# Stick-breaking attention with pooling: the closing's stores and the weight sums on GpSimd's queue, loads spread out

## The chip, the cores and the metric

One core of a Trainium2 chip. The metric is device time in microseconds; the profile beside it is one execution, recorded by the hardware profiler.

## The reference

One layer with two token mixers runs over 2048 prompt rows and 64 decode rows (each 1024 wide), everything in fp32:

```python
def merge_out(x, att, ga, pb, gb, mg, w_br_a, w_br_b, w_out):
    y_a = (att * jax.nn.silu(ga)) @ w_br_a
    y_b = (pb * jax.nn.silu(gb)) @ w_br_b
    gate = jax.nn.sigmoid(mg)
    m = gate[..., :D_MODEL] * y_a + gate[..., D_MODEL:] * y_b
    return x + m @ w_out
...
        h = rmsnorm(xp, norm_g[l])
        q, k, v, ga, u, gb, mg = split_proj(h, w_in[l])
        att = stick_breaking(...)      # 8 heads x 128, strictly causal
        pb = multi_scale_pool(...)     # trailing means of 2/4/8/16 rows minus self, a map per group
        xp = merge_out(xp, att, ga, pb, gb, mg, w_br_a[l], w_br_b[l], w_out[l])
...
    y_prompt = rmsnorm(xp, final_g)
```

`split_proj` is one projection to 8192 columns; `att` is written out as keys and values too. The change is about `merge_out`: the three products with `w_br_a`, `w_br_b` and `w_out`, and the gates.

## The kernel before

Every fp32 product is made of three products of rounded halves: `split` casts a tile to `hi` on ScalarE (L81) and takes `lo = src - hi` on VectorE (L82); TensorE then sums hi·hi, hi·lo and lo·hi (`product`, L964, L966, L968).

The program has three parts. First, projections and attention (to about 2267 us in the profile) leave three arrays in DRAM: `aT_d` and `bT_d`, the two branches' rows after their own gates, transposed, and `sm_d`, the merge gates after the sigmoid. Second, the closing (2267 to 2648): for branch i = 0 (`w_br_a`) and i = 1 (`w_br_b`), three row tiles t of 2 x 352 rows. Third, the back: `w_out` over eight pairs of 128-row blocks, residual and final norm, then the decode rows.

The three large products are done with seven block products in place of eight (Winograd's form of Strassen's scheme), p = 0 to 6, with weights `b11, b21, t2, t1, t3, b22, t4`. The `t` are sums of weight blocks: `weight_sums` loads four 128x512 pieces (`ws`, L899), subtracts four times (L902) and stores four times to `tw_d` (L903), twelve rounds in all (three weights by four k). They run beside the last projection slabs; there a planner spaces the steps of `before_closing` between slabs, and instructions of engines other than TensorE are put in an order by a scheduler. A slab is 128 columns of `w_in`: two loads `raw` (L272) of 256 KB, `whi` and `wlo` from them, 48 matmuls of 128x512 and a few narrower, and the sigmoid's stores `sm_d` (L306).

In the closing, every engine's order is written out by hand, and is the order of the code. A row tile needs `r11, r12, r21, r22` (128x4x352 each, L1044) and four sums of them. A product p is two half steps cc of 24 matmuls of 128x352 into an accumulator; a tile is 14 half steps, the closing 84 (h = 2s + cc, with s counting products). `make(s + 2)` splits the rows of the product after the next into `rhi` and `rlo`. Some results are kept by ScalarE (L979: `x1`, `x2`, `x5`); the other eight of a tile go through `emit`: add a kept result (L1103), multiply with the gate `sg` (L1105), in branch 1 add branch 0's result `mp` (L1107). The tile `sg` is then stored to `mp_d` (branch 0) or `m_d` (branch 1) by `store`, half a step later on SP (L1091), and behind it SP issues the load of `mp` for the result after the next (L1085) and of the gate four results ahead (L1078), whose tile is the one just stored. `forms` loads a weight in two pieces of 512 KB (`wraw`, two buffers, L914) and splits them; each `next(wnext)` does one piece and starts the load of the piece after the next.

In the back, a product is 12 matmuls of 128x512 and a pair has seven. `out_a` to `out_d` make the forms of a pair's rows, `join` adds results to the residual `xo` (L1204, L1205), `finish` norms and stores. `mt` and `mb` hold a pair's rows from `m_d`.

Of the kernel before, what the change touches and what calls it, by code (L numbers as in the profile page):

```python
# [15 lines left out]
P = 128  # L16
D = 1024
# [27 lines left out]
def kernel(  # L45
# [99 lines left out]
    with ExitStack() as front:  # L145
# [747 lines left out]
        def weight_sums(i):  # L893

            for k in range(4):
                t = {}
                for nm, r, c in (("b11", 0, 0), ("b12", 0, 1), ("b22", 1, 1), ("b21", 1, 0)):
                    t[nm] = kept_tile("ws").rearrange("p a b -> p (a b)")[:, 0:512]
                    nc.sync.dma_start(t[nm], weights[i][r * 512 + k * P:r * 512 + (k + 1) * P, c * 512:(c + 1) * 512])  # L899
                for j, out, x, y in ((0, "b11", "b12", "b11"), (2, "b12", "b22", "b12"),  # L900
                                     (1, "b22", "b22", "b11"), (3, "b21", "b21", "b22")):
                    nc.vector.tensor_tensor(t[out], t[x], t[y], op=ALU.subtract)  # L902
                    nc.sync.dma_start(tw_d[i, j, k * P:(k + 1) * P, :], t[out])  # L903
                yield 1.0
# [81 lines left out]
    def load_merged(n):  # L986

        r0 = pairs[n][0]
        for h in range(2):
            nc.sync.dma_start(merged[n][h], m_d[h * 512:(h + 1) * 512, r0:r0 + 256].rearrange("(k p) r -> p k r", p=P))  # L990

# [15 lines left out]
    def out_b(n, s1, s2):  # L1007
        r11, r12, r21, r22 = blocks(n)
        s1, s2 = s1[:, :, 0:P], s2[:, :, 0:P]
# [16 lines left out]
    with ExitStack() as rowx, tc.manual_schedule(engines={E.PE, E.DVE, E.Activation, E.SP}):  # L1026
# [7 lines left out]
        stores = []  # L1034

        def load_rows(s, nm):
            if s >= len(order):
                return
# [6 lines left out]

        def sum12():

            raws["s1"] = rowp.tile([P, 4, NR], F32, name="s1")
            raws["s2"] = rowp.tile([P, 4, NR], F32, name="s2")
            nc.vector.tensor_tensor(raws["s1"], raws["r21"], raws["r22"], op=ALU.add)  # L1050
            nc.vector.tensor_tensor(raws["s2"], raws["s1"], raws["r11"], op=ALU.subtract)

        def sum34():

            nc.vector.tensor_tensor(raws["r21"], raws["r11"], raws["r21"], op=ALU.subtract)
            nc.vector.tensor_tensor(raws["r12"], raws["r12"], raws["s2"], op=ALU.subtract)

        def make(s):

            if s < len(order):  # L1060
                rf[s] = row_form()
                split(rf[s][0], rf[s][1], raws[("r11", "r12", "s2", "s1", "r21", "r12", "r22")[order[s][2]]])

            elif s == len(order):
                out_a(0)
            else:
                out_b(0, rowp.tile([P, 4, NR], F32, name="s1"), rowp.tile([P, 4, NR], F32, name="s2"))
# [5 lines left out]
        def load_gate(n):  # L1073
            if n < len(leave):
                i, c, rs = where(n)
                sgs_[n] = rowp.tile([P, 2, NR], F32, name="sg", bufs=4)
# [3 lines left out]
        def load_other(n):  # L1080

            if n < len(leave) and leave[n][0]:
                i, c, rs = where(n)
                mps[n] = rowp.tile([P, 2, NR], F32, name="mp", bufs=2)
                nc.sync.dma_start(mps[n], mp_d[c * P:(c + 2) * P, rs].rearrange("(j p) r -> p j r", p=P))  # L1085

        def store():
            while stores:
                n = stores.pop(0)
                i, c, rs = where(n)  # L1090
                nc.sync.dma_start((mp_d, m_d)[i][c * P:(c + 2) * P, rs].rearrange("(j p) r -> p j r", p=P), sgs_.pop(n))  # L1091
                load_other(n + 2)
                load_gate(n + 4)
# [3 lines left out]
        def emit(src, other):  # L1097
# [3 lines left out]
            sg = sgs_[n]  # L1101
# [4 lines left out]
            if leave[n][0]:  # L1106
                nc.vector.tensor_tensor(sg, sg, mps.pop(n), op=ALU.add)  # L1107
            return n

        for nm in ("r21", "r22", "r11", "r12"):  # L1110
            load_rows(0, nm)
        for n in range(4):
            load_gate(n)
        wnext = forms(0, WFORMS[4:])
        next(wnext)
        sum12()
        for s, (i, t, p) in enumerate(order):
            r = rf.pop(s)
            if t == 2 and p == 0:
                wnext = forms(i + 1, WFORMS)  # L1120
            for cc in range(2):
# [9 lines left out]
                if cc == 1:  # L1131
                    make(s + 2)
                out = acc[:, :, 0:NR]
                n = None
                if p == 0:
                    x1[cc] = kept(out, "x1")
                elif p == 1:
                    n = emit(out, x1[cc])
# [4 lines left out]
                elif p == 4:  # L1143
                    n = emit(out, x5[cc])
                elif p == 5:
                    n = emit(out, x2[cc])
                else:
                    n = emit(out, None)
                if p == 0 and cc == 1:
                    sum34()  # L1150
                if p == 6 and cc == 1 and s + 1 < len(order):
                    sum12()
                store()
                if n is not None:
                    stores.append(n)
                if p == 4 and cc == 1:
                    for nm in ("r11", "r21", "r12") if s + 3 < len(order) else ():
                        load_rows(s + 3, nm)
                    if s + 3 == len(order):
                        merged[0] = [rowp.tile([P, 4, NR], F32, name=nm)[:, :, 0:256] for nm in ("r11", "r21")]  # L1160
                        load_merged(0)
                if p == 5 and cc == 0:
                    load_rows(s + 2, "r22")
                next(wnext, None)
        store()
        for _ in wnext:
            pass
# [3 lines left out]
    with ExitStack() as back:  # L1171
        pool = back.enter_context(tc.tile_pool(name="back", bufs=1, side="left"))
        wo = {nm: wf[2, nm] for nm in WFORMS}
        left, right, whole, cols = slice(0, 512), slice(512, 1024), slice(0, 512), slice(0, P)

        def fetch(n):
            if n < len(pairs):
                merged[n] = [pool.tile([P, 4, 256], F32, name=nm, bufs=2) for nm in ("mt", "mb")]
                load_merged(n)

        def residual(src, m):
            xt = pool.tile([P, D], F32, name="xo", bufs=4)
            nc.sync.dma_start(xt[0:m], src)
            return xt

        def finish(xt, m, dst):

            acc = [pool.tile([P, 1], F32, name=f"acc{i}", bufs=2) for i in range(4)]
            for b in range(2):
                jk = pool.tile([P, 512], F32, name="bjk", bufs=2)  # L1190
                nc.scalar.activation(jk[0:m], xt[0:m, b * 512:(b + 1) * 512], AF.Square, accum_out=acc[b][0:m])
            nc.vector.tensor_tensor(acc[0][0:m], acc[0][0:m], acc[1][0:m], op=ALU.add)
            rs = pool.tile([P, 1], F32, name="rs", bufs=2)
            rsqrt_of_mean(rs[0:m], acc[0][0:m], [acc[2][0:m], acc[3][0:m]])
            for b in range(2):
                bs = slice(b * 512, (b + 1) * 512)
                nc.vector.scalar_tensor_tensor(xt[0:m, bs], xt[0:m, bs], rs[0:m], g_bc[0:m, bs],
                                               op0=ALU.mult, op1=ALU.mult)
                nc.sync.dma_start(dst[:, bs], xt[0:m, bs])

        def join(xt, bs, ps, other):

            if other is not None:
                nc.vector.tensor_tensor(xt[:, bs], xt[:, bs], other, op=ALU.add)  # L1204
            nc.vector.tensor_tensor(xt[:, bs], ps, xt[:, bs], op=ALU.add)  # L1205

        fetch(1)
        xts = [residual(xp[pairs[0][1] + i * P:pairs[0][1] + (i + 1) * P], P) for i in range(2)]
        g_bc = pool.tile([P, D], F32, name="fg_bc")
        nc.sync.dma_start(g_bc, final_g.rearrange("(a d) -> a d", a=1).broadcast_to([P, D]))  # L1210
        for n, (_, r) in enumerate(pairs):
            f = {nm: of.pop((n, nm)) for nm in ("a11", "a12", "s2", "s1", "a22")}
            last = n + 1 == len(pairs)
            xs2 = bpsum.tile([P, 2, 512], F32, name="x")
            ys2 = bpsum.tile([P, 2, 512], F32, name="y")
            x, z, y = xs2[:, 0], ys2[:, 0], ys2[:, 1]
            product(x, f["a11"], wo["b11"], True, cols, whole)
# [87 lines left out]
```

## Time and profile before

| what | us |
|---|---|
| three runs, median (range) | 2851.36 (2848.66 to 2851.92) |
| the profiled execution | 2851.63 |
| its span | 2849.9 |
| TensorE busy in the span | 2728.8 |
| closing, first to last matmul | 2267.1 to 2648.5 |
| end of the span | 2849.9 |

The span runs from the first to the last recorded instruction. A row of a timeline gives start, length, engine, line, operation, `out<-in`, and in brackets the idle time before it with the instruction or transfer that ended it. SPq is SyncE's queue, which issues DMAs. PEclk is the clock that TensorE was granted, 1.00 being full.

### The profile page before, as it was taken

What the parts mean: (1) busy time and instruction counts of PE and PEld (TensorE: products, weight loads), DVE (VectorE), ACT (ScalarE), POOL (GpSimd) and SP (SyncE); (2) the same over time, 40 slices, a digit from 0 to 9 for tenths busy, and PEclk for the clock granted to TensorE, in tenths of its full rate; (3) what the DMA queues carried; (4) which work ended last, traced back from release to release, by engine and by line L of the source; (5) the groups of instructions that cost most, each with busy time, mean ns of one, the idle gap of its engine ahead of it and who ended that gap; (6) DMA issues with size and microseconds to landing.
All of it is one profiled execution on the core that took longest, in us unless ns stands there. A gap on an engine that the chain in (4) does not pass through costs nothing.

```text
span 2849.9 us, 41818 instructions
## 1 busy us (share of the span) xinstructions
PE 2728.8 (96%) x15052; PEld 2380.2 (84%) x15052; DVE 1848.5 (65%) x2931; ACT 1270.9 (45%) x2528; POOL 444.0 (16%) x1091
## 2 busy tenths in 40 slices
PE   6999999999999999999999999999999999798798
PEld 6989888889998988788888888887778889798686
DVE  6555555677768773678788878874444265656686
ACT  4446444455555543455555555552223132323343
POOL 2112222220000002132333333420000000000000
PEclk9999999999999999999999999999999999999899
DMA  5224222234544453211111111123369555657652
GB/s 149 70 86 123 70 73 75 82 113 149 161 154 149 148 161 119 60 53 42 54 58 52 46 56 57 35 72 101 105 225 300 196 185 168 210 171 225 209 171 92
DMA packets 360315, 343.85 MB, mean 121 GB/s; under 512 B 30174, under 2 KB 298190, under 8 KB 360108
## 3 DMA queue, kind: packets, MB, share of 16 engines
q1 hardware_dynamic: 360108, 341.19, 38.4%
q8 instruction: 118, 1.93, 0.3%
q14 instruction: 89, 0.73, 0.1%
HBM read 232.46 MB, written 108.65 MB: 120 GB/s over the span
## 4 chain that ended last, share of the span: by engine, by line
PE 81%; DMA 8%; DVE 6%; issue 2%; ACT 2%; SPq 1%; POOL 0%; DVEq 0%; ACTq 0%; POOLq 0%
PE pj L284 16%; PE pj L286 16%; PE pj L285 16%; PE tr L638 4%; PE att L655 2%; PE att L654 2%; PE z L627 2%; PE att L653 2%; PE z L626 2%; PE z L625 2%; PE x L964 2%; PE x L966 2%; PE x L968 2%; PE y L964 1%; PE y L968 1%
## 5 line engine op out<-in xcount | busy, mean ns | idle before, releaser
L284 PE MATMUL pj<-hhi,whi 128*128 128x512 f32 (+2 forms) x2608 | 946.7, 363 | 5.0 <-ACT whi L81 5.0
L286 PE MATMUL pj<-hhi,wlo 128*128 128x512 f32 (+2 forms) x2608 | 919.5, 353 | 0.5 <-DVE wlo L82 0.5
L285 PE MATMUL pj<-hlo,whi 128*128 128x512 f32 (+2 forms) x2608 | 918.0, 352 | 0.1
L284 PEld LDWEIGHTS pj<-hhi,whi 128*128 128x128 f32 x2608 | 495.3, 190 | 64.8 <-ACT whi L81 5.9
L286 PEld LDWEIGHTS pj<-hhi,wlo 128*128 128x128 f32 x2608 | 493.0, 189 | 66.8 <-DVE wlo L82 1.8
L285 PEld LDWEIGHTS pj<-hlo,whi 128*128 128x128 f32 x2608 | 494.5, 190 | 59.0 <-DVE hlo L82 0.4
L579 DVE TENSOR_TENSOR_SCAN om<-om 128x513 f32<-128x513 f32 (+3 forms) x356 | 387.5, 1088 | 213.4 <-POOL om L561 108.5
L569 ACT ACTIVATE om<-z 128x512 f32<-128x512 f32 (+2 forms) x320 | 171.6, 536 | 323.2 <-PE z L627 274.4
L82 DVE TENSOR_TENSOR wlo<-raw,whi 128x512 fp32r<-128x512 f32 x248 | 170.6, 694 | 135.5 <-ACT whi L81 134.6
L582 DVE TENSOR_TENSOR be<-be,om 128x512 f32<-128x512 f32 (+3 forms) x356 | 230.2, 647 | 31.5
L81 ACT CAST whi<-raw 128x512 fp32r<-128x512 f32 x256 | 158.1, 623 | 173.9 <-PE pj L285 135.5
L81 ACT CAST a<-tr 128x512 fp32r<-128x512 f32 (+2 forms) x356 | 188.0, 528 | 100.3 <-PE tr L638 89.6
L82 DVE TENSOR_TENSOR a<-tr,a 128x512 fp32r<-128x512 f32 (+2 forms) x356 | 215.2, 605 | 23.8 <-ACT a L81 21.6
L581 POOL COPY carry<-om 128x1 f32<-128x1 f32 x356 | 78.6, 221 | 920.7 <-DVE om L579 880.3
L638 PE MATMUL tr<-ident,be 128*128 128x128 f32 x1088 | 176.0, 274 | 6.1 <-DVE be L582 3.7
L638 PEld LDWEIGHTS tr<-ident,be 128*128 128x128 f32 x1088 | 136.5, 140 | 44.9 <-DVE be L582 8.3
L570 ACT ACTIVATE be<-z 128x512 f32<-128x512 f32 (+2 forms) x320 | 170.0, 531 | 0.0
L653 PE MATMUL att<-a,v 128*128 128x512 f32 (+1 forms) x320 | 133.4, 417 | 0.0
L574 POOL COPY om<-carry 128x1 f32<-128x1 f32 x224 | 124.0, 554 | 2.7 <-DVE be L582 0.7
L655 PE MATMUL att<-a,v 128*128 128x512 f32 (+1 forms) x320 | 118.4, 370 | 3.6 <-DVE a L82 3.3
L654 PE MATMUL att<-a,v 128*128 128x512 f32 (+1 forms) x320 | 117.3, 367 | 0.0
L627 PE MATMUL z<-khi,qlo 128*128 128x512 f32 (+2 forms) x320 | 117.1, 366 | 0.0
(313 smaller groups left out, 4544.4 us busy)
## 6 DMA issues: line engine op xcount, KB each, us to landing
raw<-in_w_in_dram SPq DMA_DIRECT2D x256, 256.0 KB, 3.2
sg<-sm_d SPq DMA_DIRECT2D x48, 352.0 KB, 3.3
kraw<-in_cache_k_dram SPq DMA_DIRECT2D x64, 256.0 KB, 3.5
vraw<-in_cache_v_dram SPq DMA_DIRECT2D x64, 256.0 KB, 2.9
sm_d<-sgm SPq DMA_DIRECT2D x48, 256.0 KB, 2.7
tw_d<-ws SPq DMA_DIRECT2D x48, 256.0 KB, 3.0
wraw<-tw_d SPq DMA_DIRECT2D x24, 512.0 KB, 4.7
out_dram<-nat SPq DMA_DIRECT2D x42, 256.0 KB, 2.3
```

The source lines that it names most:

```text
L81: nc.scalar.copy(hi, src)
L82: (nc.gpsimd if eng == "g" else nc.vector).tensor_tensor(lo, src, hi.bitcast(F32), op=ALU.subtract)
L284: nc.tensor.matmul(ps[:, 0:n], whi[:, k], hhi[:, k, c0:c0 + n], start=k == 0, stop=False)
L285: nc.tensor.matmul(ps[:, 0:n], whi[:, k], hlo[:, k, c0:c0 + n], start=False, stop=False)
L286: nc.tensor.matmul(ps[:, 0:n], wlo[:, k], hhi[:, k, c0:c0 + n], start=False, stop=k == KT - 1)
L579: nc.vector.tensor_tensor_scan(rev, rev, rev, 1.0, op0=ALU.mult, op1=ALU.bypass)
L582: nc.vector.tensor_tensor(be[:, off:512], be[:, off:512], om[:, off + 1:513], op=ALU.mult)
L627: nc.tensor.matmul(z[:, off:512], qlo[:, qs], khi[:, 0:m], start=False, stop=True)
L638: nc.tensor.transpose(tr[:, i * P:(i + 1) * P], be[:, off + j * P:off + (j + 1) * P], ident)
L653: nc.tensor.matmul(self.acc[:, s], vhi[:, js], ahi[:, s], start=first, stop=False)
L654: nc.tensor.matmul(self.acc[:, s], vlo[:, js], ahi[:, s], start=False, stop=False)
L655: nc.tensor.matmul(self.acc[:, s], vhi[:, js], alo[:, s], start=False, stop=last)
```

## The change

- `weight_sums` issues its loads and stores on GpSimd's queue instead of SP's.
- `emit` issues its own store, on GpSimd's queue, and behind it the load of `mp` two results ahead and of the gate three ahead (before: four ahead, half a step later, behind the store). There are five `sg` and three `mp` buffers (before four and two), in a pool of their own that outlives the row tiles.
- In a half step, results are kept or emitted first; `make` and the sums follow. The sums are done in place, except `s3`.
- The next tile's rows are loaded at four places of the tile: `r11` at p = 2, `r21` at p = 3, `r12` and `r22` in the two halves of p = 5 (before: three at the end of p = 4, the fourth in p = 5). At the start: three row loads, three gates, the fourth row load; the weights `t3, b22, t4` follow from half step 2.
- Weight forms are placed by half step: branch 0's last six at 5 to 10 (before from 0), branch 1's fourteen at 30 to 50 (before 28 to 41), `w_out`'s at 71 to 84.
- The row tiles are given up at half step 79; the back's first rows (`mt`, `mb`) and residuals are loaded there. `mt`, `mb` and `bjk` have one buffer, and pair n + 1's rows are fetched within pair n after `out_c` (before: two pairs ahead). The back's accumulators, and the two of the decode rows, are separate tiles. The final gains lie in two of the `sg` tiles, `s1` and `s2` in `mp` tiles.

```diff
-                    nc.sync.dma_start(t[nm], weights[i][...])
+                    nc.gpsimd.dma_start(t[nm], weights[i][...])
...
-                    nc.sync.dma_start(tw_d[i, j, k * P:(k + 1) * P, :], t[out])
+                    nc.gpsimd.dma_start(tw_d[i, j, k * P:(k + 1) * P, :], t[out])
...
+        def sum3():
+            raws["s3"] = rowp.tile([P, 4, NR], F32, name="s3")
+            nc.vector.tensor_tensor(raws["s3"], raws["r11"], raws["r21"], op=ALU.subtract)
         def sum12():
-            raws["s1"] = rowp.tile([P, 4, NR], F32, name="s1")
-            raws["s2"] = rowp.tile([P, 4, NR], F32, name="s2")
-            nc.vector.tensor_tensor(raws["s1"], raws["r21"], raws["r22"], op=ALU.add)
-            nc.vector.tensor_tensor(raws["s2"], raws["s1"], raws["r11"], op=ALU.subtract)
-        def sum34():
-            nc.vector.tensor_tensor(raws["r21"], raws["r11"], raws["r21"], op=ALU.subtract)
-            nc.vector.tensor_tensor(raws["r12"], raws["r12"], raws["s2"], op=ALU.subtract)
+            nc.vector.tensor_tensor(raws["r21"], raws["r21"], raws["r22"], op=ALU.add)
+            nc.vector.tensor_tensor(raws["r11"], raws["r21"], raws["r11"], op=ALU.subtract)
+        def sum4():
+            nc.vector.tensor_tensor(raws["r12"], raws["r12"], raws["r11"], op=ALU.subtract)
...
-        def store():
-            while stores:
-                n = stores.pop(0)
-                i, c, rs = where(n)
-                nc.sync.dma_start((mp_d, m_d)[i][...], sgs_.pop(n))
-                load_other(n + 2)
-                load_gate(n + 4)
...
             nc.vector.tensor_tensor(sg, src, sg, op=ALU.mult)
-            if leave[n][0]:
+            if i:
                 nc.vector.tensor_tensor(sg, sg, mps.pop(n), op=ALU.add)
-            return n
+            nc.gpsimd.dma_start((mp_d, m_d)[i][...], sg)
+            load_other(n + 2)
+            load_gate(n + 3)
...
+        for base, nms, at in ((2, WFORMS[4:], [5, 6, 7, 8, 9, 10]),
+                              (28, WFORMS, [30 + (8 * h) // 5 for h in range(14)]),
+                              (70, WFORMS, list(range(71, 85)))):
...
-                if cc == 1:
-                    make(s + 2)
                 out = acc[:, :, 0:NR]
...
-                if p == 4 and cc == 1:
-                    for nm in ("r11", "r21", "r12") if s + 3 < len(order) else ():
-                        load_rows(s + 3, nm)
...
+                if cc == 1:
+                    make(s + 2)
+                    if p == 0:
+                        sum4()
+                    if more and p == 5:
+                        sum3()
+                    if more and p == 6:
+                        sum12()
+                weights_at(2 * s + cc)
+                if more and (p, cc) in ((2, 0), (3, 0), (5, 0), (5, 1)):
+                    load_rows(s + 7 - p, {2: "r11", 3: "r21", 5: ("r12", "r22")[cc]}[p])
+                if not more and (p, cc) == (4, 1):
+                    rowx.close()
+                    pool = ctx.enter_context(tc.tile_pool(name="back", bufs=1, side="left"))
+                    fetch(0)
+                    xts = residuals(0)
...
+        g_bc.append(gates.tile([P, 2, NR], F32, name="fg_bc", tag="sg", bufs=5)...)
...
+    def accumulator(nm):
+        return bpsum.tile([P, 2, 512], F32, name=nm)[:, 0]
...
             join(xts[0], left, z, x1)
+            if not last:
+                fetch(n + 1)
...
-                out_b(n + 1, pool.tile([P, 4, P], F32, name="s1o"), pool.tile([P, 4, P], F32, name="s2o"))
-                fetch(n + 2)
+                out_b(n + 1)
```

The change also gives VectorE another order in the last projections. There, `ws` are the weight sums and each slab has two `wlo`. Before, from the first sum on:

```order
L902 TENSOR_TENSOR ws<-ws 128x512 x4
L82 TENSOR_TENSOR b11lo<-wraw,b11hi 128x1024
L82 TENSOR_TENSOR wlo<-raw,whi 128x512 x2
L902 TENSOR_TENSOR ws<-ws 128x512 x4
L82 TENSOR_TENSOR b11lo<-wraw,b11hi 128x1024
L902 TENSOR_TENSOR ws<-ws 128x512 x8
L82 TENSOR_TENSOR wlo<-raw,whi 128x512 x2
L82 TENSOR_TENSOR b21lo<-wraw,b21hi 128x1024 x2
L82 TENSOR_TENSOR wlo<-raw,whi 128x512 x2
L82 TENSOR_TENSOR t2lo<-wraw,t2hi 128x1024
```

And now, from the third slab behind the first sum:

```order
L82 TENSOR_TENSOR t2lo<-wraw,t2hi 128x1024
L902 TENSOR_TENSOR ws<-ws 128x512 x4
L82 TENSOR_TENSOR wlo<-raw,whi 128x512 x2
L902 TENSOR_TENSOR ws<-ws 128x512 x4
L82 TENSOR_TENSOR t2lo<-wraw,t2hi 128x1024
L82 TENSOR_TENSOR t1lo<-wraw,t1hi 128x1024
L902 TENSOR_TENSOR ws<-ws 128x512 x2
L82 TENSOR_TENSOR t1lo<-wraw,t1hi 128x1024
L82 TENSOR_TENSOR wlo<-raw,whi 128x512 x2
```

The pairs of `wlo` that followed each other with weight forms alone between them now have four to six sums between two pairs.

On SP, at the change of branch, before (`r_...` are row tiles):

```order
L1091 DMA mp_d<-sg 128x2x352
L1078 DMA sg<-sm_d 128x2x352
L1044 DMA r_25627<-bT_d 128x4x352
L1044 DMA r_25629<-bT_d 128x4x352
L1044 DMA r_25631<-bT_d 128x4x352
L914 DMA wraw<-in_w_br_b_dram 128x2x512
L1091 DMA mp_d<-sg 128x2x352
L1078 DMA sg<-sm_d 128x2x352
L1044 DMA r_25668<-bT_d 128x4x352
```

And now:

```order
L1057 DMA r_25448<-bT_d 128x4x352
L914 DMA wraw<-tw_d 128x2x512 x2
L1057 DMA r_25517<-bT_d 128x4x352
L1092 DMA sg<-sm_d 128x2x352
L914 DMA wraw<-tw_d 128x2x512
L1092 DMA sg<-sm_d 128x2x352 x2
L914 DMA wraw<-tw_d 128x2x512
L1057 DMA r_25651<-bT_d 128x4x352
L1092 DMA sg<-sm_d 128x2x352
L914 DMA wraw<-tw_d 128x2x512
L1057 DMA r_25694<-bT_d 128x4x352
```

No store stands between SP's loads any more, and the row loads are apart. On VectorE, in the last products of branch 0's first tile, before (`x_...` are kept results):

```order
L82 TENSOR_TENSOR rlo<-r_24370,rhi 128x1408
L1103 TENSOR_TENSOR x_24654<-x,x_24654 128x704
L1105 TENSOR_TENSOR sg<-x_24654,sg 128x704
L1103 TENSOR_TENSOR x_24557<-y,x_24557 128x704
L1105 TENSOR_TENSOR sg<-x_24557,sg 128x704
L82 TENSOR_TENSOR rlo<-r_24715,rhi 128x1408
L1103 TENSOR_TENSOR x_24594<-y,x_24594 128x704
L1105 TENSOR_TENSOR sg<-x_24594,sg 128x704
```

And now:

```order
L1110 TENSOR_TENSOR x_24540<-y,x_24540 128x704
L1112 TENSOR_TENSOR sg<-x_24540,sg 128x704
L82 TENSOR_TENSOR t4lo<-wraw,t4hi 128x1024
L1110 TENSOR_TENSOR x_24568<-y,x_24568 128x704
L1112 TENSOR_TENSOR sg<-x_24568,sg 128x704
L82 TENSOR_TENSOR rlo<-r_24542,rhi 128x1408
L1062 TENSOR_TENSOR s_24786<-r_24542,r_24611 128x1408
```

`rlo` moved behind the two operations that empty the accumulator of the same product.

More of the change, by code (lines that the diff above doesn't have):

```diff
@@ L1075, in load_gate @@
                 i, c, rs = where(n)
[L1076 removed]
+                sgs_[n] = gates.tile([P, 2, NR], F32, name="sg", bufs=5)
                 r0 = i * D + c * P
@@ L1118 @@
             r = rf.pop(s)
-            if t == 2 and p == 0:
-                wnext = forms(i + 1, WFORMS)
+            more = s - p + 7 < len(order)
             for cc in range(2):
@@ L1137 @@
                 elif p == 1:
-                    n = emit(out, x1[cc])
+                    emit(out, x1[cc])
                 elif p == 2:
@@ L1143 @@
                 elif p == 4:
-                    n = emit(out, x5[cc])
+                    emit(out, x5[cc])
                 elif p == 5:
-                    n = emit(out, x2[cc])
+                    emit(out, x2[cc])
                 else:
[L1148 to L1155, printed above, removed]
@@ new lines, in join @@
+    def join(xt, bs, ps, other):
+        if other is not None:
+            nc.vector.tensor_tensor(xt[:, bs], xt[:, bs], other, op=ALU.add)
+        nc.vector.tensor_tensor(xt[:, bs], ps, xt[:, bs], op=ALU.add)
+    def accumulator(nm):
+        return bpsum.tile([P, 2, 512], F32, name=nm)[:, 0]
+    for n, (_, r) in enumerate(pairs):
+        f = {nm: of.pop((n, nm)) for nm in ("a11", "a12", "s2", "s1", "a22")}
+        last = n + 1 == len(pairs)
+        x = accumulator("x")
+        product(x, f["a11"], wo["b11"], True, cols, whole)
+        x1 = kept(x, "x1")
+        z = accumulator("y")
+        product(z, f["a12"], wo["b21"], True, cols, whole)
+        out_c(n)
+        f.update((nm, of.pop((n, nm))) for nm in ("s3", "s4"))
+        join(xts[0], left, z, x1)
+        if not last:
+            fetch(n + 1)
+        product(x, f["s2"], wo["t2"], False, cols, whole)
+        x2 = kept(x, "x2")
+        y = accumulator("y")
+        product(y, f["s1"], wo["t1"], True, cols, whole)
+        x5 = kept(y, "x5")
+        if not last:
+            out_a(n + 1)
+            nxt = residuals(n + 1)
+        else:
+            both = row_form()
+            tail = [pool.tile([P, 4, 256], F32, name=nm) for nm in ("mt", "mb")]
+            for h in range(2):
+                src = m_d[h * 512:(h + 1) * 512, 1024:RA].rearrange("(k p) r -> p k r", p=P)
+                nc.sync.dma_start(tail[h][:, :, 0:DEC], src)
+                both[h] = both[h].rearrange("p a b -> p (a b)")[:, 0:512].rearrange("p (k c) -> p k c", k=4)
+                split(both[h][:, :, 0:DEC], both[h][:, :, DEC:P], tail[h][:, :, 0:DEC])
+            xt = residual(xs, DEC)
+        product(x, f["s3"], wo["t3"], False, cols, whole)
+        join(xts[1], right, x, x5)
+        product(y, f["s4"], wo["b22"], False, cols, whole)
+        join(xts[0], right, y, x2)
+        if not last:
+            out_b(n + 1)
+        product(x, f["a22"], wo["t4"], False, cols, whole)
+        join(xts[1], left, x, None)
+        if not last:
+            out_d(n + 1)
+        for i in range(2):
+            finish(xts[i], P, yp[r + i * P:r + (i + 1) * P])
+        if not last:
+            xts = nxt
```

190 lines of the change are left out of this document (73 added, 117 removed).

## The prediction

> **What bounds the kernel now.** I read the page's busy shares and its chain first, then windows over the closing and the back, then what stood ahead of each idle stretch of TensorE, then the last projections, where the weight sums run.
>
> ```profile
> PE 2728.8 (96%) x15052; PEld 2380.2 (84%) x15052; DVE 1848.5 (65%) x2931; ACT 1270.9 (45%) x2528; POOL 444.0 (16%) x1091
> PE 81%; DMA 8%; DVE 6%; issue 2%; ACT 2%; SPq 1%; POOL 0%; DVEq 0%; ACTq 0%; POOLq 0%
> ```
>
> TensorE is busy 96% of the span and is 81% of the chain: a gain can only come out of its holes. The windows (length, then busy time and count of PE, PEld, DVE, ACT, POOL, then clock, DMA share, GB/s) show where these are:
>
> ```profile
> 2299.00:2407.50 108.50, 108.31 (x676) 107.51 (x674) 58.54 (x50) 28.11 (x28) 0.00 (x0) 1.00 0.58 179
> 2267.09:2299.00 31.91, 25.25 (x142) 24.59 (x143) 15.20 (x12) 8.23 (x9) 0.00 (x0) 0.89 0.65 211
> 2407.50:2476.00 68.50, 46.57 (x258) 45.32 (x258) 40.00 (x35) 24.57 (x25) 0.00 (x0) 0.85 0.66 206
> 2523.00:2608.00 85.00, 77.14 (x454) 76.45 (x454) 51.86 (x46) 19.90 (x19) 0.00 (x0) 0.94 0.63 194
> 2608.00:2648.50 40.50, 35.33 (x197) 34.26 (x195) 28.33 (x27) 15.30 (x16) 0.00 (x0) 0.92 0.68 209
> 2690.00:2832.00 142.00, 141.80 (x626) 116.59 (x624) 110.87 (x266) 63.56 (x149) 0.00 (x0) 1.00 0.43 139
> 2648.50:2690.00 41.50, 22.02 (x65) 16.81 (x65) 23.97 (x33) 11.54 (x18) 0.00 (x0) 0.71 0.74 244
> 2835.03 0.47 PE L1265 MATMUL x<-b11hi,rhi 128*128 128x512 f32 x1 [3.23 <-DVE xo L1272]
> ```
>
> The first row is undisturbed closing. I take 0.1595 us a matmul as pace (676 are 107.8 of its 108.5 us), 3.83 a half step of 24; the undisturbed back is 142.00/626 = 0.2268, 2.72 us a product. Length minus count times pace is what a stretch loses: start 31.9 - 22.6 = 9.3; end of branch 0 with the change of branch 68.5 - 41.2 = 27.3; two tile ends 85.0 - 72.4 = 12.6; last tile 40.5 - 31.4 = 9.1; the way into the back 41.5 - 14.7 = 26.8. With 3.2 ahead of the second sum of the decode rows that is 88 us. Around the holes the granted clock is below one too (0.71 to 0.94); this slow restart lies inside these losses. The windows also show GpSimd idle (0.00).
>
> Now what the holes wait for. At the start:
>
> ```profile
> 2274.94 2.10 SPq L914 DMA_DIRECT2D wraw<-tw_d  x2
> 2277.46 1.63 DVE L1051 TENSOR_TENSOR s<-s,r 128x1408 f32<-128x1408 f32 x1 [0.24 <-DMA r<-aT_d]
> 2285.90 1.04 ACT L81 CAST t3hi<-wraw 128x1024 fp32r<-128x1024 f32 x1 [13.91 <-DMA wraw<-tw_d]
> ```
>
> The sum that product 2 needs is done at 2279.1, but ScalarE stands until 2285.90 at t3's cast, whose weights SP issued last. At the change of branch, on SP, ScalarE, VectorE and TensorE:
>
> ```profile
> 2436.76 0.46 SPq L1091 DMA_DIRECT2D mp_d<-sg  x1
> 2441.61 0.36 SPq L1078 DMA_DIRECT2D sg<-sm_d  x1
> 2442.01 2.39 SPq L1044 DMA_DIRECT2D r<-bT_d  x3
> 2449.15 1.36 ACT L81 CAST rhi<-r 128x1408 fp32r<-128x1408 f32 x1 [7.46 <-DMA r<-bT_d]
> 2450.55 1.63 DVE L82 TENSOR_TENSOR rlo<-r,rhi 128x1408 fp32r<-128x1408 f32 x1 [6.83 <-ACT rhi L81]
> 2458.38 0.63 PE L964 MATMUL x<-rhi,b11hi 128*128 128x352 f32 x1 [11.00 <-DVE sg L1105]
> SPq L1078 <- DMA mp_d<-sg: 104.0, 24, 9.4
> ```
>
> A gate load takes its tile over from a store, so SP stands 4.85 us from the store's issue to its landing; three row loads queue behind it; VectorE stands 6.83 us in front of `rlo` although a finished accumulator waits for `emit` behind it, and TensorE loses 11.00. The last row sums SP's waits of this kind on branch 0's stores: 104.0 us, 24 times, longest 9.4.
>
> **The change, part by part.** Prices (busy, mean ns; or KB, us to landing):
>
> ```profile
> L82 DVE TENSOR_TENSOR rlo<-r,rhi 128x1408 fp32r<-128x1408 f32 x28 | 45.5, 1624 | 58.8 <-ACT rhi L81 58.5
> L1105 DVE TENSOR_TENSOR sg<-x,sg 128x704 f32<-128x704 f32 x45 | 39.9, 890 | 1.2
> sg<-sm_d SPq DMA_DIRECT2D x48, 352.0 KB, 3.3
> mp_d<-sg SPq DMA_DIRECT2D x24, 352.0 KB, 4.7
> mt<-m_d SPq DMA_DIRECT2D x7, 512.0 KB, 4.7
> ```
>
> *Start.* Rows and gates come ahead of all weights, and t3's cast no longer stands before product 2's rows. One more sum of 1.6 (`sum3`) precedes: rows at 2277, three sums to 2281, cast 1.36, `rlo` 1.62: about 2284, where product 2 is due two products (15.3) after 2267.1, at 2282.4. Loss 1.5 of 9.3: saves 7.8.
>
> *`emit` ahead of `make`.* An accumulator's release no longer waits for a cast and an `rlo` nor for the loads under them; `make` is now delayed by `emit`'s two or three operations of 0.89, which is hidden because it serves the product after the next, 7.7 us later. If that cover went, 1.8 to 2.7 us a product would show. The sums of a tile keep their number.
>
> *Stores on GpSimd, gates three ahead.* SP loses 48 stores and its standing for them; a tile's row loads go out one by one, 2 to 7 half steps before their sums or casts (7.7 us at the least). A store may take 2 half steps (7.7) before SP meets it at the tile's next load, and 5 half steps less a gate load, 19.1 - 3.3 = 15.8, before an `emit` is late. GpSimd-issued stores are not in this trace; nearest are SP's 4.7. Bounds: no dearer, or twice, 9.4, still inside 15.8. I take no cost. With branch 1's 14 half-forms over 21 half steps, the 39.9 us of the middle (27.3 + 12.6) should go; I keep 3 for single late loads: saves 37.
>
> *Last tile and junction.* Here w_out's 14 half-forms stay one to a half step:
>
> ```profile
> 2658.42 1.04 ACT L81 CAST b22hi<-wraw 128x1024 fp32r<-128x1024 f32 x1 [5.65 <-DMA wraw<-in_w_out_dram]
> 2661.21 1.22 DVE L82 TENSOR_TENSOR b22lo<-wraw,b22hi 128x1024 fp32r<-128x1024 f32 x1
> 2677.30 0.69 DVE L1012 TENSOR_TENSOR s1o<-mt,mb 128x512 f32<-128x512 f32 x1 [4.48 <-DMA mb<-m_d]
> 2681.13 0.80 PE L964 MATMUL y<-t1hi,rhi 128*128 128x512 f32 x1 [7.98 <-DVE xo L1205]
> ```
>
> Pair 1's rows, the residuals and the final gains were requested only once the closing's tiles were free; now pair 0's rows and residuals land within the last tile, the gains behind it. But the tile stays crowded. VectorE: 22 operations of 0.89, 14 weight `lo` of 1.22, 5 `rlo` of 1.62, nine of 0.69 are 19.6 + 17.1 + 8.1 + 6.2 = 51 of its 53.6 us. DMA: 14 weights of 512 KB, 8 stores and 11 gates and `mp` of 352, rows and residuals of 2 MB are about 16 MB, 300 GB/s, where this kernel's best stretch moves 299 (a row below). I leave 14 of the 35.9 us (9.1 + 26.8): saves 22. In the back, rows are fetched one pair ahead into one buffer, about 6 us before their first sum against 4.7 to land: cost 0, bound 1.5 us in 7 pairs, 10. One `bjk` and accumulators by product only shorten what each holds; the window's 110.87 of 142.00 on VectorE hides them. The decode rows' two accumulators save 3.
>
> *Weight sums on GpSimd.* They run beside the last projections:
>
> ```profile
> 2095.90:2240.00 144.10, 139.12 (x589) 111.30 (x588) 60.67 (x84) 38.73 (x61) 0.00 (x0) 0.99 0.92 299
> 2150.00:2240.00 90.00, 90.00 (x389) 72.98 (x388) 37.16 (x54) 22.36 (x38) 0.00 (x0) 1.00 0.90 298
> 2097.62 2.87 DVE L902 TENSOR_TENSOR ws<-ws 128x512 f32<-128x512 f32 x4 [4.17 <-DMA ws<-in_w_br_a_dram]
> 2107.46 2.97 DVE L902 TENSOR_TENSOR ws<-ws 128x512 f32<-128x512 f32 x4 [2.79 <-DMA ws<-in_w_br_a_dram]
> 2116.15 2.87 DVE L902 TENSOR_TENSOR ws<-ws 128x512 f32<-128x512 f32 x4 [2.23 <-DMA ws<-in_w_br_a_dram]
> L903 SPq DMA_DIRECT2D tw_d<-ws x48: 319/326/1228, 2098.3 to 2235.4; - x48
> 2131.36 4.42 SPq L272 DMA_DIRECT2D raw<-in_w_in_dram x3
> 2129.28 0.50 PE L284 MATMUL pj<-hhi,whi 128*128 128x512 f32 x1 [4.42 <-ACT whi L81]
> ```
>
> Pace here is 90.00/389 = 0.2314 us, 11.1 a slab of 48 matmuls; of 144.1 us 589 matmuls need 136.3, so 7.8 are lost around the hole of 4.42, where raw loads stood behind `tw_d` stores on SP. That hole goes. But VectorE's new order puts more sums ahead of each slab's `wlo`: the slab that follows the 32nd sum before follows the 44th now. It starts seven slabs before 2267.1, near 2190. From 2097.6 that leaves 93 us for 11 rounds of four loads, sums and stores: 8.5 a round. Before, the nearest rounds took 9.8 and 8.7, but the stage as a whole (2235.4 - 2098.3)/12 = 11.4, with the DMA engines 92% busy, and the bytes do not change. At 8.5 nothing is lost; at 11.4, 11 x 2.9 = 32, less the share that the waiting projections leave to the sums, about a third: 21. I take 10.3 a round, 20 less a fifth: 16, so with the 7.8 a net loss of 8, between a gain of 8 and a loss of 13.
>
> The Trainium skill, "DMA: Bandwidth & Descriptors", section "Issuing engines are not separate DMA queues", says that transfers issued elsewhere still run on the same 16 engines and only the issuing sequencer's time is saved. The 0.92 agrees; by it a round stays as long as its bytes take, 11.4, and the sum would end 5 later.
>
> **Sum.** 7.8 + 37 + 22 + 3 - 8 = 62. The profiled execution took 2851.63, 0.3 above the median 2851.36: 2790 from either.
>
> **Rivals.** (a) The sums keep up (8.5 to 9 a round) and the junction closes to 6: 62 + 16 + 8 = 86, 2766. For it, the two nearest rounds; against, 92% DMA. (b) A slow GpSimd queue, 13 a round: 11 x 4.5 = 50 instead of 16, gain 28, 2824. (c) Single-buffered rows stall each pair by 1.5 and the last tile keeps its 36: 62 - 10 - 22 = 30, 2822. For it, the 51 of 53.6; against, the junction's chain of late requests is gone. (d) Slower than before: GpSimd pays a price for each transfer that paces the rounds, eight to a round. Without loss in the stage the gain is 62 + 16 = 78, so it decides where 11 rounds lose 78: 8.5 + 7.1 = 15.6 a round, 1.95 us a transfer; at 17 it ends at 2868. For it, no row shows GpSimd issuing a transfer; against, SP pays 0.33 and the engine is otherwise idle.
>
> The same page, "Anatomy of one DMA", gives a GpSimd-issued transfer 2.0 us plus bytes over 436 GB/s. If these ran one after the other a round would be 8 x 2.6 = 21, an estimate from the page by which it would be slower, 2910; no run here shows such a transfer, and the page does not say that they cannot overlap.
>
> **How the numbers follow.** Forecast 0.5 (2776 to 2806), (a) 0.17, (b) 0.13, (c) 0.12, (d) 0.05, no change 0.03. 0.2% (5.7 us) is about what a measurement of this kernel can tell from no change. The range 2768 to 2826 leaves out (d), no change and half of (a). Faster 0.92, same 0.03, slower 0.05.
>
> **What would show it.** Right: SP's gate loads without waits for stores; no TensorE hole from half step 34 to the last tile; the closing's first hole under 2 us; one or more holes of 10 to 20 us in all at `whi` or `wlo` in the last projections, with `ws` ahead of them on VectorE; a junction shorter but not gone, waiting for weights. Wrong: stores landing beyond 15 us, `ws` loads landing far later than before, or a hole in each pair of the back that waits for `mt` or `mb`.

## The result and the profile after

The changed kernel takes 2805.61 us (median of four runs, 2802.82 to 2815.53) against 2850.45 of the kernel before beside it: ratio 0.9849, interval 0.9824 to 0.9874, 44.8 us faster. The forecast was 2790, range 2768 to 2826. The profiled execution is the slowest of the four, 2815.53; every row of the changed kernel below is from it, and its sum is made against the profiled 2851.63 of before.

The windows, in the columns of the prediction:

```profile
2095.90:2265.00 169.10, 144.17 (x586) 113.94 (x586) 59.80 (x84) 38.04 (x61) 49.65 (x92) 0.93 0.77 254
2292.12:2311.00 18.88, 17.57 (x107) 17.04 (x108) 8.19 (x6) 4.23 (x4) 0.00 (x0) 1.00 0.91 311
2311.00:2614.00 303.00, 303.00 (x1885) 302.86 (x1884) 215.40 (x191) 105.14 (x102) 32.14 (x45) 1.00 0.69 228
2617.50:2655.00 37.50, 26.31 (x96) 20.87 (x95) 25.39 (x38) 14.75 (x25) 1.43 (x2) 0.82 0.66 230
2655.00:2797.00 142.00, 137.00 (x594) 111.85 (x593) 105.75 (x252) 58.60 (x141) 0.00 (x0) 0.99 0.42 137
```

For 303 us of the closing TensorE has no hole (busy 303.00, clock 1.00). The start loses 18.9 - 17.1 = 1.8, the way into the back 37.5 - 21.8 = 15.7, the pairs 142.0 - 134.7 = 7.3. The first row is new: in the last projections 586 matmuls need 135.6 at 0.2314, so 33.5 us are lost where before it was 7.8. Rows of TensorE's timeline (idle in brackets), one or two for each place that loses, and the closing's first matmul:

```profile
2151.57 0.80 PE L284 MATMUL pj<-hhi,whi 128*128 128x512 f32 x1 [12.13 <-ACT sgm L302]
2210.72 0.80 PE L286 MATMUL pj<-hhi,wlo 128*128 128x512 f32 x1 [5.05 <-DVE wlo L82]
2292.12 0.40 PE L964 MATMUL x<-rhi,b11hi 128*128 128x352 f32 x1 [0.78 <-issue]
2309.37 0.43 PE L966 MATMUL x<-rlo,t2hi 128*128 128x352 f32 x1 [1.23 <-DVE rlo L82]
2625.56 0.77 PE L964 MATMUL x<-b11hi,rhi 128*128 128x512 f32 x1 [7.08 <-DVE sg L1112]
2637.44 0.80 PE L964 MATMUL x<-t2hi,rhi 128*128 128x512 f32 x1 [4.11 <-ACT x L979]
2741.52 0.50 PE L964 MATMUL x<-t2hi,rhi 128*128 128x512 f32 x1 [2.13 <-ACT x L979]
```

The closing begins at 2292.12, 25.0 us later than before (2267.09); from there to the first matmul of the back it takes 2625.56 - 2292.12 = 333.4 instead of 2656.62 - 2267.09 = 389.5, so 56.1 less; from there to the end of the span 187.9 instead of 193.3, 5.4 less. 56.1 + 5.4 - 25.0 = 36.5, the difference of the two spans (2849.9 - 2813.5 = 36.4) but for rounding.

SP's waits for store landings, and GpSimd's transfers (count, KB each, median us from issue to landing; then the stores of the sums: shortest, median and longest issue in ns, first and last start):

```profile
SPq L1092 <- DMA mp_d<-sg: 50.7, 11, 12.6
SPq L1092 <- DMA m_d<-sg: 17.0, 10, 3.6
mp_d<-sg POOLq DMA_DIRECT2D x24, 352.0 KB, 4.3
m_d<-sg POOLq DMA_DIRECT2D x24, 352.0 KB, 5.8
L903 POOL DMA_DIRECT2D tw_d<-ws x48: 540/545/548, 2100.8 to 2235.4; - x48
```

SP still stands for landings at its gate loads, 50.7 + 17.0 = 67.7 us (104.0 + 70.6 = 174.6 before), and TensorE has no hole from it.

The rounds of the weight sums are counted from the first sum of one to the first sum of the next, on VectorE. Before, the fourth and the fifth begin, then the last; changed, the first and the last:

```profile
2124.42 0.69 DVE L902 TENSOR_TENSOR ws<-ws 128x512 f32<-128x512 f32 x1 [5.39 <-DMA ws<-in_w_br_a_dram]
2154.88 1.41 DVE L902 TENSOR_TENSOR ws<-ws 128x512 f32<-128x512 f32 x2
2230.38 0.69 DVE L902 TENSOR_TENSOR ws<-ws 128x512 f32<-128x512 f32 x1 [4.06 <-DMA ws<-in_w_out_dram]
```

```profile
2099.85 1.42 DVE L902 TENSOR_TENSOR ws<-ws 128x512 f32<-128x512 f32 x2 [6.91 <-DMA ws<-in_w_br_a_dram]
2231.05 0.69 DVE L902 TENSOR_TENSOR ws<-ws 128x512 f32<-128x512 f32 x1 [6.04 <-issue]
```

The eleven steps before are 2230.38 - 2097.62 = 132.8 us, but one of them, 30.5, is a pause between the fourth and the fifth round; the other ten take 10.2 each. The changed kernel has no such pause, and its eleven steps take (2231.05 - 2099.85)/11 = 11.9 each.

### The profile page after: what moved, and what is told of

Read it like the earlier page. It is cut to its first block, busy times and chain, and to the rows that moved or that the text cites. A ratio compares the mean times of both kernels' runs of the same rounds, so it can differ in the third digit from the quotient of the medians.

```text
span 2813.5 us, 41919 instructions
## 1 busy us (share of the span) xinstructions
PE 2717.3 (97%) x15052; PEld 2369.7 (84%) x15052; DVE 1849.0 (66%) x2931; ACT 1269.7 (45%) x2528; POOL 529.4 (19%) x1235
## 4 chain that ended last, share of the span: by engine, by line
PE 83%; DMA 7%; DVE 6%; issue 2%; ACT 2%; POOL 1%; SPq 0%; DVEq 0%; POOLq 0%; ACTq 0%
PE pj L284 15%; PE pj L286 15%; PE pj L285 15%; PE tr L638 4%; PE x L964 3%; PE x L968 3%; PE x L966 3%; PE att L655 2%; PE att L654 2%; PE att L653 2%; PE z L627 2%; PE z L626 2%; PE z L625 2%; PE y L964 2%; PE y L968 2%
## 5 line engine op out<-in xcount | busy, mean ns | idle before, releaser
L561 POOL TENSOR_SCALAR_AFFINE_SELECT om<-om 128x128 f32<-128x128 f32 x128 | 50.7, 396 | 354.3 <-ACT om L569 354.2
```

## The experiments

The times are medians. "Start" is the closing's first matmul, "closing" the time from it to the back's first matmul, both of the profiled execution; at the prediction's pace of 0.1595 the closing's 2016 matmuls take 321.5.

| kernel | us | ratio to before (interval) | start | closing |
|---|---|---|---|---|
| before (medians beside each run) | 2847.8 to 2850.5 | 1 | 2267.09 | 389.5 |
| changed | 2805.61 | 0.9849 (0.9824 to 0.9874) | 2292.12 | 333.4 |
| e1_sums_sp | 2781.18 | 0.9766 (0.9751 to 0.9780) | 2266.49 | 328.1 |
| e2_before_sums_pool | 2876.28 | 1.0102 (1.0086 to 1.0117) | 2294.08 | 384.9 |
| e3_sums_sp_early | 2792.64 | 0.9806 (0.9790 to 0.9822) | 2277.79 | 328.6 |
| e4_no_pool | 2781.15 | 0.9763 (0.9748 to 0.9777) | 2266.52 | 330.2 |
| e5_pool_no_tw | 2810.25 | 0.9867 (0.9852 to 0.9882) | 2294.97 | 328.9 |
| e6_make_first | 2779.22 | 0.9757 (0.9742 to 0.9771) | 2267.32 | 332.2 |
| e7_forms_dense | 2784.47 | 0.9770 (0.9753 to 0.9786) | 2268.06 | 331.0 |
| e8_rows_late | 2783.30 | 0.9771 (0.9757 to 0.9786) | 2267.24 | 332.1 |
| e9_gate4_sp | 2808.72 | 0.9863 (0.9849 to 0.9878) | 2267.00 | 359.3 |
| e10_junction | 2782.00 | 0.9768 (0.9751 to 0.9784) | 2266.01 | - |
| e11_best | 2775.47 | 0.9748 (0.9733 to 0.9764) | 2260.27 | 324.5 |
| e12_before_gates5 | 2809.26 | 0.9860 (0.9843 to 0.9878) | 2266.41 | 351.1 |

**The weight sums' queue.** First the sums alone, undone and done.

```diff
 # e1_sums_sp (on the changed kernel); e2_before_sums_pool is the reverse, on the kernel before
-                    nc.gpsimd.dma_start(t[nm], weights[i][...])
+                    nc.sync.dma_start(t[nm], weights[i][...])
...
-                    nc.gpsimd.dma_start(tw_d[i, j, ...], t[out])
+                    nc.sync.dma_start(tw_d[i, j, ...], t[out])
```

> The changed kernel with the weight sums back on SP's queue, and so with VectorE's old order in the last projections. Theory (order): the 25.0 us by which the closing begins later (2292.1 against 2267.1) come from the sums standing ahead of the slabs' wlo; they go, the closing begins at 2267 to 2270 and the kernel ends 14 to 25 us earlier than the changed one, 2780 to 2791. Rival (the closing's gain needs the early sums, or the later start only hides loads that were late anyway): the closing's first product starts earlier but new holes appear in branch 0, total 2800 or more.

> The kernel before with one edit, the weight sums on GpSimd's queue; everything from the closing on as before. Theory (the move costs by itself): the closing begins 12 to 25 us later and the kernel takes 2862 to 2876. Rival (the loss is a matter of the whole change, such as the pools' layout): 2850 to 2855.

Both came out the way of the first theory: 24.4 us gained by undoing it, inside its 14 to 25; 28.5 lost by doing it alone (2876.3 against 2847.8), at the upper edge of its 2862 to 2876. The start of the closing moves by 25.6 (to 2266.49) and by 27.0 (to 2294.08), the latter beyond the expected 25. So this part of the change is a loss of some 25 us by itself, and all the rest together a gain of 66.6 (2847.8 - 2781.2).

Why it loses: the order, or GpSimd's queue? e3 keeps SP's queue and puts the sums earlier.

```diff
 # e3_sums_sp_early (on e1_sums_sp)
-            (before_closing(), 25.0))
+            (before_closing(), 40.0))
```

> As e1_sums_sp, but the planner's pace of the sums' steps is raised from 25 to 40, which puts 44 sums ahead of the 17th wlo (before: 32 to 36; the changed kernel: 44 ahead of the 15th), on SP's queue. Theory (order): rounds still take some 11 us, so TensorE stands at wlo much as in the changed kernel and the closing begins 8 to 25 us later than in e1_sums_sp. Rival (GpSimd's queue itself is the price: 0.54 us an issue, longer landings): SP carries the early order, the closing begins within 4 us of e1_sums_sp.

```profile
2131.90 0.80 PE L284 MATMUL pj<-hhi,whi 128*128 128x512 f32 x1 [15.59 <-ACT whi L81]
2277.79 0.40 PE L964 MATMUL x<-rhi,b11hi 128*128 128x352 f32 x1 [0.78 <-issue]
L903 SPq DMA_DIRECT2D tw_d<-ws x48: 319/323/1607, 2098.3 to 2221.2; - x48
2095.90:2250.00 154.10, 138.51 (x585) 111.00 (x584) 62.09 (x84) 39.80 (x61) 0.00 (x0) 0.94 0.84 280
```

The rows are TensorE's one large hole, the start, the sums' stores and the stage. An early order costs 11.3 us of start on SP's queue too, a number inside the theory's 8 to 25; the stage loses 154.1 - 585 x 0.2314 = 18.7. But the theory's mechanism did not show: 15.59 of it lies in one hole ahead of `whi`, for which a `raw` load stood behind sums on SP, and no other hole reaches 0.8. From first sum to first sum the rounds took 9.8 here, outside one pause of 22.5. Where the changed kernel's holes come from, e5 asks.

```diff
 # e5_pool_no_tw (on the changed kernel)
-            if nm[0] == "t":
+            if i == 0 and nm in ("t2", "t1"):
+                src = weights[0][0:512, 0:512]
+            elif nm[0] == "t":
                 src = tw_d[i, int(nm[1]) - 1]
```

> The changed kernel, but branch 0's weight forms t2 and t1 are made from the block b11 of w_br_a instead of the stored sums (t2 and t1 hold other values; times and sizes of the work stay). In the changed kernel ScalarE stands 18.7 us at t2's second cast, since its load waits for the stores of all 16 sums of w_br_a; the sigmoid behind it keeps the accumulator, and TensorE loses its longest hole, 12.1 us. Theory (this wait on the stores is the larger half of the loss): that hole and the small ones behind it go, the closing begins at 2272 to 2282 instead of 2292. Rival (VectorE's sums ahead of wlo, my prediction's step, hold TensorE whatever ScalarE waits for): the hole comes back at wlo, the closing begins at 2288 or later.

In the changed kernel ScalarE stands at `t2hi` with the sigmoid behind it; in e5 that wait is gone, and TensorE's two longest holes are at `wlo` (holes of 1 to 4 us behind the sigmoid are left, 11 in all). The first two rows are of the changed kernel, the others of e5:

```profile
2149.97 1.05 ACT L81 CAST t2hi<-wraw 128x1024 fp32r<-128x1024 f32 x1 [18.69 <-DMA wraw<-tw_d]
2150.92 0.59 ACT L302 ACTIVATE sgm<-pj 128x512 f32<-128x512 f32 x1
```

```profile
2176.82 2.87 DVE L902 TENSOR_TENSOR ws<-ws 128x512 f32<-128x512 f32 x4 [7.29 <-DMA ws<-in_w_br_b_dram]
2180.34 0.50 PE L286 MATMUL pj<-hhi,wlo 128*128 128x512 f32 x1 [4.19 <-DVE wlo L82]
2210.67 2.14 DVE L902 TENSOR_TENSOR ws<-ws 128x512 f32<-128x512 f32 x3 [5.95 <-DMA ws<-in_w_out_dram]
2213.47 0.80 PE L286 MATMUL pj<-hhi,wlo 128*128 128x512 f32 x1 [8.73 <-DVE wlo L82]
2294.97 0.40 PE L966 MATMUL x<-rhi,b11hi 128*128 128x352 f32 x1 [0.78 <-issue]
```

The rival was right: the start is 2294.97 and the total within the changed kernel's runs. With that wait gone, the loss comes back where VectorE's sums stand ahead of `wlo`. What stays open is how the loss is shared between the order and the rounds. The sums on GpSimd, with the order that comes with them, begin the closing 25.6 to 28.5 us later (the changed kernel, e2, e5), the early order on SP 11.3. GpSimd's rounds were longer in every run, 11.9 to 12.2 on average, where SP's took 9.8 to 10.6 outside their pause in all the other kernels with twelve rounds; no run had GpSimd's rounds with SP's order.

**The closing's stores.**

```diff
 # e4_no_pool (on e1_sums_sp)
-            nc.gpsimd.dma_start((mp_d, m_d)[i][...], sg)
+            nc.sync.dma_start((mp_d, m_d)[i][...], sg)
```

> As e1_sums_sp, with the closing's stores on SP too, at the same place in emit: nothing is issued by GpSimd. Theory (the spread loads and emit ahead of make carry the gain of the middle, the store's queue little): up to 8 us slower than e1_sums_sp. Rival (the queue carries it, since SP stands at each store for the sum and at each gate for a landing with row loads behind it): holes of 20 to 40 us in the closing.

No difference (0.9763 and 0.9766): beside the other parts, the closing's queue that gave the change its name is worth nothing. SP stands at the stores for VectorE instead:

```profile
SPq L1115 <- DVE sg L1112: 95.6, 21, 17.2
SPq L1115 <- DVE sg L1114: 76.3, 22, 15.9
```

That is 172 us of standing, as much as the 174.6 before for landings (the branch 0 row of the prediction and 70.6 in branch 1), and it costs nothing. Next, the order and the spread, each undone alone on e1_sums_sp:

```diff
 # e6_make_first
+                if cc == 1:
+                    make(s + 2)
                 out = acc[:, :, 0:NR]
...
                 if cc == 1:
-                    make(s + 2)
 # e7_forms_dense
-                              (28, WFORMS, [30 + (8 * h) // 5 for h in range(14)]),
+                              (28, WFORMS, list(range(29, 43))),
 # e8_rows_late
-                if more and (p, cc) in ((2, 0), (3, 0), (5, 0), (5, 1)):
-                    load_rows(s + 7 - p, {2: "r11", 3: "r21", 5: ("r12", "r22")[cc]}[p])
+                if more and (p, cc) in ((4, 1), (5, 0)):
+                    for nm in ("r11", "r21", "r12") if p == 4 else ("r22",):
+                        load_rows(s + 7 - p, nm)
```

> As e1_sums_sp, with make ahead of emit again. Theory (with the loads spread, rows are there in time, so the order costs little): 0 to 8 us slower than e1_sums_sp. Rival (the order carries the gain of the middle: a finished accumulator waits for a cast and an rlo): holes ahead of b11 at each of the tile ends, 15 to 35 us slower.

> As e1_sums_sp, with branch 1's fourteen weight forms one to a half step from 29 to 42 as before. Theory (they crowd the tile in which the branch changes): 5 to 15 us slower, by holes between half steps 33 and 43. Rival (with SP free of landings the loads come in time anyway): within 3 us.

> As e1_sums_sp, with the next tile's rows loaded where they were before, three at the end of p = 4 and the fourth in p = 5. Theory (late rows were the cause of the holes at each tile's end, since VectorE stands at rlo with emit behind it): a hole of 2 to 6 us at each of five tile ends, 10 to 30 us slower. Rival (with emit ahead of make a late row is hidden): within 4 us.

e6 is not slower at all (0.9757; the closing has holes of 0.6 to 0.7 us at three tile ends and is 4 us longer in its trace). e7 and e8 are 2 to 3 us slower in the median, about 1 by the ratio, with intervals that overlap e1's. The theories on e7 and e8 are refuted, that on e6 held. With the other parts in place, none of the three is worth more than that.

**The gate's tile.** What remained is how long after a store its tile is loaded again.

```diff
 # e9_gate4_sp (on e4_no_pool)
-                sgs_[n] = gates.tile([P, 2, NR], F32, name="sg", bufs=5)
+                sgs_[n] = gates.tile([P, 2, NR], F32, name="sg", bufs=4)
...
-            load_gate(n + 3)
+            load_gate(n + 4)
...
-        for n in range(3):
+        for n in range(4):
             load_gate(n)
 # e12_before_gates5 (on the kernel before)
-                sgs_[n] = rowp.tile([P, 2, NR], F32, name="sg", bufs=4)
+                sgs_[n] = rowp.tile([P, 2, NR], F32, name="sg", bufs=5)
```

> As e4_no_pool (nothing issued by GpSimd), with four gate buffers and the gate loaded four results ahead, into the tile whose store SP has just issued, as before the change. Spread loads and the order of emit and make stay. Theory (what the changed kernel gained in the middle is that a gate load no longer waits for the landing of the store just issued; each other part alone is worth 0 to 3 us): SP stands 4 to 5 us at each of the 48 gate loads again, rows and weights come late, 10 to 35 us slower than e4_no_pool. Rival (the parts replace each other; the spread loads hide SP's standing): within 5 us.

> The kernel before with one number changed: five gate buffers instead of four. Each gate load (four results ahead, behind the store on SP) then takes over the tile of the store one result earlier, not of the one just issued. All else as before. e9_gate4_sp lost 27 us by going the other way. Theory (waiting for the store just issued is sufficient as a cause): SP's waits for store landings fall from 174 us to under 60, the holes from half step 33 to the last tile shrink, 15 to 30 us faster than before. Rival (it must come with the spread loads or with emit ahead of make): under 8 us.

e9 loses 27.6 us against e4 with everything else of e4 in place, inside its theory's 10 to 35. e12 gains 40.5 on the kernel before with one number changed, more than the 15 to 30 that its theory had. SP's waits at the gate loads, first e9, then e12:

```profile
SPq L1092 <- DMA mp_d<-sg: 92.4, 24, 7.2
SPq L1092 <- DMA m_d<-sg: 63.8, 20, 6.1
```

```profile
SPq L1078 <- DMA mp_d<-sg: 18.7, 10, 4.5
SPq L1078 <- DMA m_d<-sg: 8.6, 5, 2.7
2439.95 0.60 PE L964 MATMUL x<-rhi,b11hi 128*128 128x352 f32 x1 [3.00 <-DVE sg L1105]
2617.50 0.77 PE L964 MATMUL x<-b11hi,rhi 128*128 128x512 f32 x1 [7.18 <-DVE sg L1105]
```

174.6 us of waiting become 27.3, and the 11.00 us hole at the change of branch becomes 3.00. e12 keeps late rows, dense forms, `make` ahead of `emit` and stores on SP. So the wait of a load for the store issued just before it is a sufficient cause of more than half of what the closing lost, and its return costs 27.6 with the rest in place (e9). It is not the whole. The closing before takes 389.5 - 321.5 = 68.0 more than its matmuls need; the buffer alone removes 38.4 of it (e12, 351.1), the rest of the change, without the buffer and the two queues, 30.2 (e9, 359.3), both 59.3 (e4, 330.2). In total time, too, e9 without the fifth buffer is 2848.4 - 2808.7 = 39.7 faster than before, about as much as e12. Which of the other parts bring this without the buffer was not run; start, last tile and way into the back are among them.

SP's stand for VectorE's sum in e4 does no harm; the likely reason is that it ends when the result is there, where a landing comes 4 to 5 us after that, at each result, with the row and weight loads behind.

**A better version.** Two rearrangements on e1_sums_sp.

```diff
 # e10_junction
-                              (70, WFORMS, list(range(71, 85)))):
+                              (70, WFORMS, list(range(71, 81)) + [82, 83])):
...
+                if s == 41 and cc == 0:
+                    out_a(0)
+                    xts = residuals(0)
...
+        if n == 0:
+            next(wnext[0])
...
+            (nc.gpsimd if n else nc.sync).dma_start(merged[n][h], m_d[...])
 # e11_best (on e10_junction)
-            yield from weight_sums(2)
+            if 12 <= h < 28 and h % 2 == 0:
+                (sums_make if h % 4 == 2 else sums_load)((h - 12) // 4)
...
-            (before_closing(), 25.0))
+            (before_closing(), 17.0))
```

`sums_load` and `sums_make` are one round of `weight_sums(2)`, in two `wraw` tiles.

> As e1_sums_sp, with the way into the back rearranged: pair 0's residuals are loaded three half steps later, its first split comes behind the emit of half step 82 instead of ahead of it, w_out's b22 forms come behind the last two emits and t4's within pair 0 (a22 of pair 0 in two gate tiles), and the back's rows are loaded on GpSimd's queue. In e1_sums_sp TensorE stands 6.0 and 5.0 us at the junction, since VectorE stands at a split that waits for rows and then at weights, with emit behind, and 1 to 2 us in a few pairs where a row load stands behind a residual's on SP. Theory: the holes shrink to under 3 us together, 8 to 14 us faster than e1_sums_sp. Rival (the DMA engines are full there, so the loads are as late in any order): within 4 us.

> As e10_junction, with w_out's weight sums taken out of the last projections and done in branch 0's second tile (two wraw tiles a round, stores on GpSimd), and the planner's pace of the remaining steps lowered from 25 to 17, which puts 8 instead of 16 sums ahead of the slab that stands in e1_sums_sp. Theory (a third of the sums' 25 MB leaves a stretch in which the DMA engines are 92% busy; the second tile has 5 us a half step of idle VectorE time per tile at least and a DMA share of 0.58): the hole of 4 us with its slow restart goes, 4 to 8 us faster than e10_junction. Rival (the closing's second tile pays for it): no faster than e10_junction, with holes between half steps 14 and 30.

e10 gains nothing, as its rival had it: the holes are 3.37, 0.77, 1.99 and in a pair 2.57 us where e1 had 6.01, 4.95 and 1.89, but the total is the same, and why it does not follow is open. Its VectorE row shows why a hole stayed, a load of `mp` that lands late:

```profile
2593.79 0.89 DVE L1117 TENSOR_TENSOR sg<-sg,mp 128x704 f32<-128x704 f32 x1 [4.01 <-DMA mp<-mp_d]
```

e11 is the fastest of all, 6.5 us below e10 in the median, inside the expected 4 to 8, with overlapping intervals. The last projections lose 137.1 - 580 x 0.2314 = 2.9 with a DMA share of 0.76 (e1: 0.92), and the second tile is without a hole:

```profile
2095.90:2233.00 137.10, 135.37 (x580) 108.19 (x579) 50.68 (x68) 37.30 (x60) 0.00 (x0) 1.00 0.76 250
2307.00:2370.00 63.00, 63.00 (x396) 63.00 (x395) 46.26 (x47) 15.70 (x15) 15.71 (x26) 1.00 0.86 292
```

## Why the prediction was right, and where it was not

The sign, the range and the places were right; the sum was 62 where the profiled execution shows 36 and the medians 45. That the median 2805.61 is inside the forecast's own 2776 to 2806 is by a hair, and so partly luck: the profiled execution is outside it.

- *Start*: saved 9.3 - 1.8 = 7.5, forecast 7.8.
- *Middle*: no hole is left of the 39.9, forecast 37. The reason given was half wrong. The store's queue, which headed the term, is worth nothing (e4); the fifth buffer that stood beside it, "gates three ahead", is the largest single cause (e9, e12). That VectorE stands at `rlo` with `emit` behind it was a true reading of the row, but only the place where lateness showed: with the lateness gone, the order costs nothing (e6). The sign "SP's gate loads without waits for stores" did not come (67.7 us are left), but no hole follows from it.
- *Last tile and junction*: saved 35.9 - 15.7 = 20.2, as the last tile lost nothing measurable; forecast 22. The residual sits where it was forecast, at late weights and rows, as ScalarE's rows show. That order alone does not cure it is shown by e10. The decode rows' hole of 3.23 is gone, as forecast (3).

```profile
2618.14 0.62 ACT L81 CAST rhi<-mt 128x512 fp32r<-128x512 f32 x1 [7.45 <-DMA mt<-m_d]
2628.43 1.04 ACT L81 CAST b22hi<-wraw 128x1024 fp32r<-128x1024 f32 x1 [5.08 <-DMA wraw<-in_w_out_dram]
```

- *Back*: forecast 0 with a bound of 10; it lost 7.3, rival (c)'s stall in smaller form. The single buffer's landing of 6 us was judged against its own load time only. SP stands 34.6 us for residual tiles in this kernel (their stores' landings), and the row loads queue behind it. It stood 31.6 there before as well, with rows fetched two pairs ahead and nothing lost, so the likely reason is the shorter lead; no run tried the second buffer.

```profile
SPq L995 <- DMA out_dram<-xo: 34.6, 12, 4.5
2696.82 0.69 DVE L1026 TENSOR_TENSOR s<-mt,mb 128x512 f32<-128x512 f32 x1 [3.56 <-DMA mb<-m_d]
```

- *Weight sums*: the step that failed by size. It was forecast as a net loss of 8 (at most 13); it measured 33.5 - 7.8 = 25.7 by the stage's rows, 25.0 at the closing's start, and e1 against the changed kernel gives 24.4. The term took 10.3 a round where GpSimd's rounds took 11.9, between the forecast and rival (b)'s 13. Its upper end of 11.4 was misread: (2235.4 - 2098.3)/12 counts twelve steps between first and last store where there are eleven, and one of these is the pause of 30.5. Outside it SP's rounds took 10.2, so 10.3 was right for SP's queue, and what failed is the assumption that a round costs the same on GpSimd's queue, in the order that comes with it, where it was 1.7 longer. A forecast with 11.9 would have been 11 x (11.9 - 8.5) = 37 undiscounted and 30 less a fifth; 33.5 was lost in all, so the discount is neither borne out nor refuted. Eight issues of 0.54 in place of 0.33 would make 1.7 too, an estimate that no run isolates. The longest hole, 12.13, stood behind ScalarE's `t2hi`, a wait that the prediction did not name; without it the loss stays (e5).
- *The rule of the Trainium skill* ("DMA: Bandwidth & Descriptors", "Issuing engines are not separate DMA queues") says that another issuing engine saves the issuing sequencer's time alone; e4 (no difference) agrees. The weight sums do not bear out what I made of it, a round of 11.4 on either queue.
- *The price of the Trainium skill* in the same page, "Anatomy of one DMA", 2.0 us plus bytes over 436 GB/s, would have been 21 a round if run in a row, an estimate from the page. The 11.9 measured shows that these transfers overlap, since four loads of 5.2 and four stores of 3.0 us to their landing would be 33 in a row. Their stores in the closing land in 4.3 and 5.8, against 4.7 and 4.5 before and 3.2 and 3.9 from SP in e4.

## What to carry to other kernels

When a load reuses the tile of a store that its own queue has just issued, each such load stops the queue for a landing; one more buffer gained as much here (40.5) as all the rest of the change without it and without the two queues (39.7), and it should be tried first and alone. Moving work that other instructions are ordered against can move those instructions too: compare the order of the engines that feed the bound, and measure rounds from start to start, with pauses apart, before a stage's mean is taken as their price. Undo each part of a compound change alone before crediting it; here one part cost 25 us, and much of the buffer's gain was credited to a queue and an order that were worth nothing beside it.

## What the runs showed that I had not expected

A GpSimd-issued transfer occupies its engine for 0.54 us (256 KB) to 0.72 us (352 KB), where SP's issues of the same transfers take 0.33 and 0.36 (e4). And in e4 SP stands for 172 us of a closing of 330 us without costing anything, waiting for results of VectorE.
